# When the row sums of a gated feed-forward layer enter GpSimd's queue: at once, or two TensorE products later

## The chip, the cores and the metric

The kernel runs on one core of a Trainium2 chip. The metric is the time of one execution on the device in microseconds (us). TensorE multiplies matrices out of the on-chip memory SBUF into PSUM banks; VectorE (DVE), ScalarE (ACT) and GpSimd (POOL) do the elementwise work; SyncE (SP) and GpSimd issue most of the DMA transfers to and from HBM. Each engine takes its own instructions in order; between engines semaphores make one wait for another.

## The reference

One layer of a trunk over 2048 tokens of width 1024, in float32:

```python
xn = rmsnorm(x, norm1_g)
z = xn @ w_in                        # pooling branch, HGRN2 branch, gates
...
x = x + merged @ w_o
x = x + conv_glu_ffn(rmsnorm(x, norm2_g), w_up, conv_w, conv_b, w_down)
return rmsnorm(x, final_g)

def conv_glu_ffn(x, w_up, conv_w, conv_b, w_down):
    h = x @ w_up                     # 1024 -> 2 x 2816
    hp = pad(h, CONV_WIDTH - 1)      # two tokens of history
    hc = sum(conv_w[j] * hp[:, j:j + S] for j in range(3)) + conv_b
    val, gate = split(hc, 2)
    return (silu(gate) * val) @ w_down
```

The change is in the last part, the feed-forward layer (up-projection, causal convolution over three tokens, SiLU gate, down-projection).

## The kernel before

**Blocks and halves.** The tokens are worked off in two blocks of 1024 (`b0` = 0 and 2 in the names: `h0_...`, `h2_...`). Each block goes first through the mixer (input projection, pooling, HGRN2, output projection), then through the feed-forward layer. There a block is two halves of 512 tokens, `hf` 0 and 1. Channels lie on the 128 partitions, tokens along the free axis, so one tile is 128 x 512.

**Units and products.** The up-projection has 22 units per block; unit `m` makes 128 channels of the value (`s` = 0) and the same 128 of the gate (`s` = 1) for both halves. These four tiles form a 2 x 2 matrix product, done with seven products in place of eight (Strassen's way), in the order P1, P6, P5, P7, P2, P4, P3. A product is twelve matmuls of 128 x 512: four steps along the width, each with three terms, because both operands are split into a high and a low part. Three PSUM banks hold them: X takes P1 and P2, Z takes P6, P7 and P4, V takes P5 and P3. Products add up in a bank, and in between partial results are read out: after P1 ScalarE copies X to `e1` (L992); after P6 VectorE makes `u2` = `e1` - Z (L994), and P7, which goes on adding in Z, waits for that read; after P7 `u3` = Z - `e1` (L998). The four tiles `h(s,hf)` come out as h(1,1) after P7 (VectorE, L958), h(0,0) after P2 (ScalarE, L952), h(1,0) after P4 (L956) and h(0,1) after P3 (VectorE, L958).

**Behind a tile.** `conv` takes `h(s,hf)`: GpSimd copies the two columns that lie before it, the halo (L1339: from the history if `hf` is 0, otherwise from the end of half 0) and, with `hf` 1, its own last two columns into the history (L1341). ScalarE starts `e` with the token's own weight and the bias (L1344), and VectorE adds the first and the second tap, the tokens one and two places earlier (L1346, L1348). `glu` makes the gated row: SiLU on ScalarE (L1352), then the product on VectorE (L1354 for half 1, L1356 for half 0; for units 0 to 3 the half-0 product is GpSimd's, since `G_POOL` is 4). `glu(0)` runs after P4, `glu(1)` after P3.

**Sums of rows.** The down-projection is again done with seven products, over pairs of units `k` = m // 2. Its seven operands are three gated rows themselves (P1: half 1 of the even unit; P2: half 1 of the odd unit; P4: half 0 of the odd unit) and four sums of rows, P7, P5, P6, P3, which `add_forms` makes on GpSimd (L1064, tiles `gf{b0}_{P}_{k}`): P7 once the even unit is complete, P5 and P6 (= P5 minus a row) behind the odd unit's first half, P3 (= P6 plus a row) behind its second. Each is stored to HBM (`dg...`): the sums by a DMA from GpSimd's queue right behind each sum (L1368), the rows by a list that SP works off at the next product. The down-projection fetches them back through GpSimd's queue (`g...`, L776) and splits each into a high and a low part (`dn_P_kh` by L577 on ScalarE, `dn_P_kl` by L578 on VectorE); its first steps are split while the last unit still runs.

**What sets the order.** `up_order` puts units 0 and 1, and 2 and 3, next to one another, product by product (the head pairs); units 4 to 21 follow one after another. Weights come as raw tiles by SP (8 buffers) and are split by L204 on ScalarE and L205 on VectorE up to four tiles ahead. A scheduler of the framework simulates the program and gives each engine its final order from the order in which the code issues instructions and from dependencies; so code that is issued later may come later on the engine, among whatever is ready. `in_turn(ins)` gives an instruction a dependency for this scheduling alone, on the latest matmul: in the scheduler's order it comes after that matmul, and no semaphore is waited for in the program.

All matmuls are recorded at one line (L145). The engine rows name tiles without their buffer numbers: `up_Z`, `h`, `e`, `gf_P`, `dg_P`, `ops` (a split weight tile), `raw` (a loaded one).

Of the kernel before, what the change touches and what calls it, by code (L numbers as in the profile page):

```python
# [69 lines left out]
N_RAW = 8  # L70
GROUP = 4
SUM_LAG = 7
N_OPS = 6
LOOKAHEAD = 4
MM_PER_TICK = 6
# [3 lines left out]
def tile_trunk(  # L79
# [16 lines left out]
    pe, act, dve, pool, sp = nc.tensor, nc.scalar, nc.vector, nc.gpsimd, nc.sync  # L96
# [3 lines left out]
    rawp = ctx.enter_context(tc.tile_pool(name="rawp", bufs=N_RAW))  # L100
    opsp = ctx.enter_context(tc.tile_pool(name="opsp", bufs=N_OPS))
    slots = ctx.enter_context(tc.tile_pool(name="slots", bufs=N_SLOTS))
# [138 lines left out]
    class Sums:  # L241
# [12 lines left out]
        def make(self, g):  # L254
# [4 lines left out]
            for dst, src, add in (("s1", 2, 0), ("s3", 2, 0), ("s1", 3, 1), ("s3", 0, 1),  # L259
# [4 lines left out]
                else:  # L264
                    with tc.issue_after(stream.mark.ins):
                        act.dma_start(self.t[g, dst], x)
                yield SUM_LAG
            self.done.add(g)
# [158 lines left out]
    sums = {}  # L427
# [627 lines left out]
                        step(j, k, ws[n])  # L1055
                stream.used(hold)

    def add_forms(two, forms, k, name, store=lambda p, t: None):

        def comb(p, x0, x1, op):  # L1060
            if (p, k) in forms or x0 is None or x1 is None:
                return
            t = slot(f"{name}_{p}_{k}")
            pool.tensor_tensor(t, x0, x1, op)  # L1064
            forms[p, k] = t
            store(p, t)

        for p, at in (("P1", (1, 0)), ("P2", (1, 1)), ("P4", (0, 1))):
            if (p, k) not in forms and at in two:
                forms[p, k] = two[at]  # L1070
                store(p, two[at])
        comb("P7", two.get((1, 0)), two.get((0, 0)), ALU.subtract)
        comb("P5", two.get((0, 0)), two.get((0, 1)), ALU.subtract)
        comb("P6", forms.get(("P5", k)), two.get((1, 0)), ALU.subtract)
        comb("P3", forms.get(("P6", k)), two.get((1, 1)), ALU.add)
# [247 lines left out]

    def ffn(b0, forms, late):
        gd, gt, gp = {}, {}, {}
        stores = []

        def flush():
            for d, g in stores:
                sp.dma_start(d, g)  # L1330
            stores.clear()

        def emit_up(m):
            hs, ts = {}, {}

            def conv(s, hf):
                mt = m + MF * s
                h = hs[s, hf]
                pool.tensor_copy(h[:, 0:2], hist[:, mt] if hf == 0 else hs[s, 0][:, TB : TB + 2])  # L1339
                if hf == 1:  # L1340
                    pool.tensor_copy(hist[:, mt], h[:, TB : TB + 2])  # L1341
                t = slot(f"e{b0}_{m}_{s}_{hf}")
                ts[s, hf] = t
                act.activation(t, h[:, 2:], AF.Identity, bias=col(o_cb + mt),  # L1344
                               scale=col(o_cw + 4 * MF + mt))
                dve.scalar_tensor_tensor(t, h[:, 1 : 1 + TB], col(o_cw + 2 * MF + mt), t,  # L1346
                                         ALU.mult, ALU.add)
                dve.scalar_tensor_tensor(t, h[:, 0:TB], col(o_cw + mt), t, ALU.mult, ALU.add)  # L1348

            def glu(hf):  # L1350
                g = ts[1, hf]
                act.activation(g, g, AF.Silu)  # L1352
                if hf:
                    dve.scalar_tensor_tensor(g, g, -1.0, ts[0, hf], ALU.mult, ALU.mult)  # L1354
                else:
                    (pool if m < G_POOL else dve).tensor_tensor(g, g, ts[0, hf], ALU.mult)  # L1356
                k = m // 2
                two = gp.setdefault(k, {})
                two[hf, m % 2] = g

                def store(p, t):
                    name = f"dg{b0}_{p}_{k}"
                    d = dram.tile([P, TB], F32, tag=name, name=name)
                    gd[p, k] = d
                    if p in R_FORM:
                        stores.append((d, t))
                    else:
                        pool.dma_start(d, t)  # L1368

                add_forms(two, gt, k, f"gf{b0}", store)  # L1370

            def emit(s, hf, a, ps):
                h = slot(f"h{b0}_{m}_{s}_{hf}", 2 + TB)
                hs[s, hf] = h
                value(h[:, 2:], a, ps)
                first = (0, 0) if m >= 2 * N_HEADS else (1, 0)
                if (s, hf) == first:
                    conv(0, 0)
                if (s, hf) == (1, 0):
                    conv(1, 0)  # L1380
                    glu(0)
                elif (s, hf) == (0, 1):
                    conv(0, 1)
                    conv(1, 1)
                    glu(1)

            return emit

        acc = {}
        fg = []  # L1390
        fss = {}

        def load_acc(which):
            for hf, c in which:
                for j in range(NT):
                    acc[hf, j, c] = fetch(x2d[b0 + hf, j, c], f"ac{b0}_{hf}_{j}_{c}", pool)

        def square(hf, j, c):
            if (hf, j) not in fss:
                fss[hf, j] = small.tile([P, 4], F32, tag="fss", name=f"fss{b0}_{hf}_{j}")  # L1400
            act.activation(slot(f"fj{b0}_{hf}_{j}_{c}"), acc[hf, j, c], AF.Square,
                           accum_out=fss[hf, j][:, c : c + 1])

        def final(hf, j):
            if hf == 1 and not last:
                yield FIN_WAIT
            for c in range(2):
                square(hf, j, c)
            halves = [acc.pop((hf, j, c)) for c in range(2)]
            res = [slot(f"fo{b0}_{hf}_{j}_{c}") for c in range(2)]  # L1410
            ss = fss[hf, j]
            pool.tensor_tensor(ss[:, 2:3], ss[:, 0:1], ss[:, 1:2], ALU.add)
            r = rstd_of(ss[:, 2:3], 1, 1.0 / D, f"f{b0}_{hf}_{j}r")
            yield 3
            rr = (b0 + hf) * TB + j * P
            for c in (1 - hf, hf):
                if (hf, c) == (0, 1):
                    act.activation(res[c], halves[c], AF.Copy, scale=r[:, 0:1])
                    pool.tensor_tensor(res[c], res[c], fg[c], ALU.mult)
                else:  # L1420
                    dve.scalar_tensor_tensor(res[c], halves[c], r[:, 0:1], fg[c],  # L1421
                                             ALU.mult, ALU.mult)
                sp.dma_start(out[rr : rr + P, 512 * c : 512 * c + 512], res[c])

        down = Rows(f"dn{b0}", "dn", DOWN, MF // 2,
                    lambda p, k: fetch(gd[p, k], f"g{b0}_{p}_{k}", pool), acc, 5)
        EARLY = {"P7": 2, "P4": 3}
        units = {}
        for n, (m, p) in enumerate(up_order()):
            if n == GO_AT:  # L1430
                go_up[0] = True
            if m not in units:
                units[m] = Unit(f"up{b0}_{m}", "up", emit_up(m))
            u = units[m]
            u.multiply(p, forms, late)
            if p != "P3":
                flush()
            u.after(p)
            if m == MF - 1 and p in EARLY:
                down.make(EARLY[p])  # L1440

        last = b0 + 2 >= SEQ // TB
        nxt = []

        def each0(k):
            if k in (3, 5, 7):
                load_acc((((1, 1), (0, 0), (0, 1))[(k - 3) // 2],))

        def each1(k):
            if k == 5:  # L1450
                load_acc(((1, 0),))

        def each2(k):
            if k == 2:
                for h in range(2):
                    t = slot(f"fg{b0}_{h}")
                    sp.dma_start(t, final_g[512 * h : 512 * h + 512].partition_broadcast(P))
                    fg.append(t)

        def each3(k):  # L1460
            if k == X_AT and not last:
                load_rows(b0 + 2)
                nxt.append(forms_of("x", b0 + 2, o_n1, go=lambda: go_io[0]))
            if k == X_AT2 and not last:
                load_rows(b0 + 3)

        down.make(3)
        flush()
        down.run("P1", 0, each0)
        down.run("P6")  # L1470
        down.run("P2", 0, each1)
        down.run("P7")
        down.run("P5", 0, each2)
        down.run("P4", 2, done=lambda j: Task(final(0, j)))
        go_io[0] = False
        down.run("P3", 6 if last else 3, each3, lambda j: Task(final(1, j)))
        return nxt[0] if nxt else None
# [15 lines left out]
    for b in range(0, SEQ // TB, 2):  # L1493
        forms, task, late = nxt
        join(task)
        forms, task, late = mixer(b, forms, late)
# [52 lines left out]
```

## Time and profile before

| | |
|---|---|
| time, median of 3 runs | 2761.86 us (2761.05 to 2764.86) |
| profiled execution, its own time | 2769.87 us |
| its span | 2767.9 us |
| mean granted clock of TensorE | 0.969 |
| bytes moved | 515.75 MB, mean 186 GB/s |
| sums of rows (L1064), mean of one | 1.328 us (two rows), 1.311 us (a sum and a row) |
| halo copies (L1339), mean of one | 0.534 us, x88 |
| stores of the sums (`dg_P<-gf_P`) | x88, 256 KB, 2.7 us from issue to landing |

The profiled execution lies 2.0 us above its span: that is what stands before the first and behind the last recorded instruction. A line of the page's list of groups reads: line, engine, operation, out<-in (partitions x elements, type), count | busy time, mean ns of one | idle time of the engine just before these instructions, and who ended most of it. In a timeline row the first two numbers are start and duration in us (with `xN` at the end: N instructions together), and the bracket at the end is the idle time before it and who released it.

### The profile page before, as it was taken

The numbers are of one execution on the slowest core, as the hardware profiler recorded it, in microseconds if no ns is written. First come the engines' busy times: TensorE is split into PE (matmuls) and PEld (weight loads), VectorE is DVE, ScalarE is ACT, GpSimd is POOL, SyncE is SP. The second block draws the span as 40 slices with busy tenths as digits, with TensorE's granted clock in tenths as the row PEclk, the third lists the DMA queues.
The fourth block names the chain that finished last, engine by engine and source line by source line (L and its number), as shares of the span: only waits on it lengthen the run. The fifth ranks groups of instructions, "written<-read, shape, count | busy, mean of one in ns | idle before, by whom it ended". The sixth has DMA issues, their size and how long they took to land. (4 is left out here: it accounts for less than half of the span.)

```text
span 2767.9 us, 35412 instructions
## 1 busy us (share of the span) xinstructions
PE 2581.0 (93%) x11464; PEld 2085.2 (75%) x11464; DVE 1932.8 (70%) x3390; ACT 1166.4 (42%) x2204; POOL 907.0 (33%) x1273
## 2 busy tenths in 40 slices
PE   7899999889979999989989999999998899998998
PEld 5677887667767777767868788888776677776886
DVE  6888878368876766666577787775877666667744
ACT  5333434224534444434464344442354444444533
POOL 5544343072443233343252111202333322224412
PEclk8999999999989999999999999999999999999999
DMA  5656666879677787899888444346343443435943
GB/s 201 212 145 166 173 167 184 259 235 262 159 184 200 204 217 222 222 298 351 257 239 240 124 122 130 121 153 236 123 138 101 128 127 124 141 119 175 345 148 103
DMA packets 258313, 515.75 MB, mean 186 GB/s; under 512 B 26224, under 2 KB 42736, under 8 KB 257648
## 3 DMA queue, kind: packets, MB, share of 16 engines
q1 hardware_dynamic: 177600, 301.01, 33.8%
q0 software_dynamic: 51040, 129.52, 19.5%
q10 hardware_dynamic: 29488, 82.96, 8.5%
q8 instruction: 90, 1.47, 0.2%
q14 instruction: 95, 0.78, 0.1%
HBM read 422.69 MB, written 206.05 MB: 227 GB/s over the span
## 5 line engine op out<-in xcount | busy, mean ns | idle before, releaser
L204 ACT CAST ops<-raw 128x512 fp32r<-128x512 f32 x732 | 451.5, 620 | 951.6 <-PE dn_P L145 161.3
L205 DVE TENSOR_TENSOR ops<-raw,ops 128x512 fp32r<-128x512 f32 x732 | 534.4, 733 | 324.0 <-ACT ops L204 312.6
L1344 ACT ACTIVATE e<-h,cols 128x512 f32<-128x512 f32 x176 | 138.5, 812 | 45.4 <-DVE h L958 38.4
L1346 DVE SCALAR_TENSOR_TENSOR e<-h,cols,e 128x512 f32<-128x512 f32 x176 | 130.9, 765 | 31.9 <-POOL h L1339 21.5
L1348 DVE SCALAR_TENSOR_TENSOR e<-h,cols,e 128x512 f32<-128x512 f32 x176 | 129.9, 752 | 0.6
L776 POOL DMA_DIRECT2D g_P<-dg_P x154 | 85.1, 558 | 136.7 <-PE dn_P L145 76.8
L1064 POOL TENSOR_TENSOR gf_P<-e,e 128x512 f32<-128x512 f32 x44 | 58.4, 1328 | 193.5 <-DVE e L1354 128.1
L145 PE MATMUL up_Z<-m_T30h,ops 128*128 128x512 f32 x88 | 42.1, 478 | 77.1 <-DVE up_u L994 77.1
L998 DVE TENSOR_TENSOR up_u<-up_Z,up_e 128x512 f32<-128x512 f32 x44 | 30.4, 691 | 116.5 <-PE up_Z L145 116.5
L1339 POOL COPY h<-h 128x2 f32<-128x2 f32 x88 | 45.9, 534 | 154.1 <-DVE h L956 154.1
L145 PEld LDWEIGHTS up_Z<-m_T30h,ops 128*128 128x128 f32 x88 | 18.0, 205 | 93.7 <-DVE up_u L994 76.3
L1064 POOL TENSOR_TENSOR gf_P<-gf_P,e 128x512 f32<-128x512 f32 x44 | 57.7, 1311 | 85.0 <-DVE e L1354 84.6
L1273 POOL TENSOR_TENSOR ya<-ya,gl 128x512 f32<-128x512 f32 x32 | 46.2, 1473 | 111.8 <-DVE gl L1265 110.3
L1341 POOL COPY hist<-h 128x2 f32<-128x2 f32 x88 | 28.1, 319 | 167.1 <-DVE h L958 166.9
L1206 ACT ACTIVATE gt<-gt,cols 128x512 f32<-128x512 f32 x48 | 34.8, 725 | 78.6 <-DVE gt L958 60.1
L1352 ACT ACTIVATE e<-e 128x512 f32<-128x512 f32 x88 | 55.2, 627 | 29.3 <-DVE e L1348 28.2
L1040 DVE TENSOR_TENSOR ac<-ac,dn_P 128x512 f32<-128x512 f32 x72 | 46.7, 683 | 27.4 <-PE dn_P L145 20.1
L825 POOL COPY qm<-q 128x64 f32<-128x64 f32 x64 | 25.5, 411 | 121.3 <-DVE q L849 25.0
L1169 POOL TENSOR_TENSOR q<-q,qs 128x512 f32<-128x512 f32 x16 | 21.9, 1367 | 128.8 <-ACT qs L1168 78.0
L958 DVE TENSOR_TENSOR h<-up_u,up_V 128x512 f32<-128x512 f32 x88 | 60.1, 683 | 2.8 <-PE up_V L145 2.3
L1040 DVE TENSOR_TENSOR x<-x,wo_P 128x512 f32<-128x512 f32 x88 | 55.9, 676 | 7.2 <-PE wo_P L145 7.2
L952 ACT COPY h<-up_X 128x512 f32<-128x512 f32 x44 | 25.8, 587 | 80.0 <-PE up_X L145 80.0
(1270 smaller groups left out, 8382.0 us busy)
## 6 DMA issues: line engine op xcount, KB each, us to landing
g_P<-dg_P POOLq DMA_DIRECT2D x154, 256.0 KB, 7.0
raw<-in_w_up_t SPq DMA_DIRECT2D x132, 256.0 KB, 3.0
raw<-in_w_in_t SPq DMA_DIRECT2D x98, 256.0 KB, 2.9
dg_P<-gf_P POOLq DMA_DIRECT2D x88, 256.0 KB, 2.7
raw<-in_w_io SPq DMA_DIRECT2D x68, 256.0 KB, 5.3
dg_P<-e SPq DMA_DIRECT2D x66, 256.0 KB, 3.2
raw<-in_w_dn SPq DMA_DIRECT2D x66, 256.0 KB, 5.4
x<-in_x SPq DMA_DIRECT2D x64, 256.0 KB, 5.4
```

What stands on the lines that cost most here:

```text
L145: count[1] = pe.matmul(*args, **kw)
L204: self.mark = act.copy(hi, v)
L205: dve.tensor_tensor(lo, v, f32(hi), ALU.subtract)
L776: eng.dma_start(t, d)
L958: dve.tensor_tensor(dst, t, ps, ALU.add if how == "add" else ALU.subtract)
L1040: dve.tensor_tensor(t, t, ps[j], ALU.add if sg > 0 else ALU.subtract)
L1064: pool.tensor_tensor(t, x0, x1, op)
L1273: pool.tensor_tensor(y[m, hf], y[m, hf], g, ALU.add)
L1344: act.activation(t, h[:, 2:], AF.Identity, bias=col(o_cb + mt), scale=col(o_cw + 4 * MF + mt))
L1346: dve.scalar_tensor_tensor(t, h[:, 1 : 1 + TB], col(o_cw + 2 * MF + mt), t, ALU.mult, ALU.add)
L1348: dve.scalar_tensor_tensor(t, h[:, 0:TB], col(o_cw + mt), t, ALU.mult, ALU.add)
L1352: act.activation(g, g, AF.Silu)
```

## The change

The rows P1, P2 and P4 are entered and their stores listed at once as before. The four sums, with the stores behind them, are put on a list and issued two products later (`FORM_LAG`), right after the matmuls of that product are issued, each sum pinned by `in_turn` behind the last of these matmuls in the scheduler's order. `have` is a copy of the pair's rows as they were when the sums were put off, so that the same sums are made at each place. What is left on the list after the last unit is issued there. `add_forms` has another caller (other operands of the layer), which passes neither argument and so works as before.

```diff
 SUM_LAG = 7
+FORM_LAG = 2
...
-    def add_forms(two, forms, k, name, store=lambda p, t: None):
+    def add_forms(two, forms, k, name, store=lambda p, t: None, sums=True, pin=lambda i: None):
 
         def comb(p, x0, x1, op):
             if (p, k) in forms or x0 is None or x1 is None:
                 return
             t = slot(f"{name}_{p}_{k}")
-            pool.tensor_tensor(t, x0, x1, op)
+            pin(pool.tensor_tensor(t, x0, x1, op))
             forms[p, k] = t
             store(p, t)
...
                 store(p, two[at])
+        if not sums:
+            return
         comb("P7", two.get((1, 0)), two.get((0, 0)), ALU.subtract)
...
     def ffn(b0, forms, late):
         gd, gt, gp = {}, {}, {}
+        later, turn = [], [0]
         stores = []
...
-                add_forms(two, gt, k, f"gf{b0}", store)
+                have = dict(two)
+                add_forms(have, gt, k, f"gf{b0}", store, False)
+                later.append((turn[0] + FORM_LAG, lambda: add_forms(
+                    have, gt, k, f"gf{b0}", store, True, in_turn)))
...
             u.multiply(p, forms, late)
+            turn[0] = n
+            while later and later[0][0] <= n:
+                later.pop(0)[1]()
             if p != "P3":
                 flush()
             u.after(p)
...
+        for _, fn in later:
+            fn()
         last = b0 + 2 >= SEQ // TB
```

Behind the change the line numbers are shifted: L1339 becomes L1343, L1341 L1345, L1064 L1065, L1346 L1350, L1348 L1352, L1354 L1358, L1356 L1360, L1368 L1372, L958 L959, L994 L995, L205 L206.

On GpSimd, around the end of unit 9 in the second block (names are `h2_9_0_1`: block, unit, value or gate, half; the tail is a buffer number). Before:

```order
L1339 COPY h2_9_1_1_20302<-h2_9_1_0_20345 128x2
L1064 TENSOR_TENSOR gf2_P5_4_20355<-e2_8_1_0_20180,e2_9_1_0_20348 128x512
L1368 DMA dg2_P5_4_20357<-gf2_P5_4_20355 128x512
L1064 TENSOR_TENSOR gf2_P6_4_20359<-gf2_P5_4_20355,e2_8_1_1_20213 128x512
L1339 COPY h2_9_0_1_20380<-h2_9_0_0_20321 128x2
L1341 COPY hist_121<-h2_9_0_1_20380 128x2
L1368 DMA dg2_P6_4_20361<-gf2_P6_4_20359 128x512
L1064 TENSOR_TENSOR gf2_P3_4_20397<-gf2_P6_4_20359,e2_9_1_1_20390 128x512
L1368 DMA dg2_P3_4_20399<-gf2_P3_4_20397 128x512
```

and now:

```order
L1343 COPY h2_9_1_1_20302<-h2_9_1_0_20345 128x2
L1343 COPY h2_9_0_1_20372<-h2_9_0_0_20321 128x2
L1345 COPY hist_121<-h2_9_0_1_20372 128x2
L1065 TENSOR_TENSOR gf2_P5_4_20407<-e2_8_1_0_20180,e2_9_1_0_20348 128x512
L1372 DMA dg2_P5_4_20409<-gf2_P5_4_20407 128x512
L1065 TENSOR_TENSOR gf2_P6_4_20411<-gf2_P5_4_20407,e2_8_1_1_20213 128x512
L1372 DMA dg2_P6_4_20413<-gf2_P6_4_20411 128x512
L1065 TENSOR_TENSOR gf2_P3_4_20437<-gf2_P6_4_20411,e2_9_1_1_20382 128x512
L1372 DMA dg2_P3_4_20439<-gf2_P3_4_20437 128x512
```

The halo copy of the value's second half, `h2_9_0_1`, and the history copy behind it stood behind sums P5 and P6; now they stand ahead of P5.

On VectorE, at the same place, from the product of the first half to `u2` of unit 10. Before:

```order
L1356 TENSOR_TENSOR e2_9_1_0_20348<-e2_9_1_0_20348,e2_9_0_0_20324 128x512
L205 TENSOR_TENSOR ops649_20450<-raw635_20255,ops649_20450 128x512
L958 TENSOR_TENSOR h2_9_0_1_20380<-up2_9_u2_20263,up2_9_V_20265 128x512
L1346 SCALAR_TENSOR_TENSOR e2_9_0_1_20384<-h2_9_0_1_20380,cols_84,e2_9_0_1_20384 128x512
L1346 SCALAR_TENSOR_TENSOR e2_9_1_1_20390<-h2_9_1_1_20302,cols_84,e2_9_1_1_20390 128x512
L205 TENSOR_TENSOR ops650_20467<-raw636_20275,ops650_20467 128x512
L1348 SCALAR_TENSOR_TENSOR e2_9_0_1_20384<-h2_9_0_1_20380,cols_84,e2_9_0_1_20384 128x512
L1348 SCALAR_TENSOR_TENSOR e2_9_1_1_20390<-h2_9_1_1_20302,cols_84,e2_9_1_1_20390 128x512
L205 TENSOR_TENSOR ops651_20488<-raw637_20292,ops651_20488 128x512
L1354 SCALAR_TENSOR_TENSOR e2_9_1_1_20390<-e2_9_1_1_20390,e2_9_0_1_20384 128x512
L994 TENSOR_TENSOR up2_10_u2_20441<-up2_10_e1_20421,up2_10_Z_20423 128x512
```

and now, from the read of bank V on:

```order
L959 TENSOR_TENSOR h2_9_0_1_20372<-up2_9_u2_20263,up2_9_V_20265 128x512
L1352 SCALAR_TENSOR_TENSOR e2_9_1_0_20348<-h2_9_1_0_20345,cols_84,e2_9_1_0_20348 128x512
L206 TENSOR_TENSOR ops648_20426<-raw634_20230,ops648_20426 128x512
L1350 SCALAR_TENSOR_TENSOR e2_9_0_1_20376<-h2_9_0_1_20372,cols_84,e2_9_0_1_20376 128x512
L1350 SCALAR_TENSOR_TENSOR e2_9_1_1_20382<-h2_9_1_1_20302,cols_84,e2_9_1_1_20382 128x512
L1352 SCALAR_TENSOR_TENSOR e2_9_0_1_20376<-h2_9_0_1_20372,cols_84,e2_9_0_1_20376 128x512
L1360 TENSOR_TENSOR e2_9_1_0_20348<-e2_9_1_0_20348,e2_9_0_0_20324 128x512
L1352 SCALAR_TENSOR_TENSOR e2_9_1_1_20382<-h2_9_1_1_20302,cols_84,e2_9_1_1_20382 128x512
L206 TENSOR_TENSOR ops649_20450<-raw635_20251,ops649_20450 128x512
L206 TENSOR_TENSOR ops650_20467<-raw636_20275,ops650_20467 128x512
L1358 SCALAR_TENSOR_TENSOR e2_9_1_1_20382<-e2_9_1_1_20382,e2_9_0_1_20376 128x512
L995 TENSOR_TENSOR up2_10_u2_20441<-up2_10_e1_20417,up2_10_Z_20419 128x512
```

The read of bank V (`h2_9_0_1`), both first taps of the second half (L1350) and one second tap now come before the product of the first half (L1360, formerly L1356), and the weight tiles `ops649` and `ops650` now stand behind them.

On GpSimd, in the first head pair (units 0 and 1) of the second block. Before:

```order
L1339 COPY h2_1_1_1_18945<-h2_1_1_0_18995 128x2
L1356 TENSOR_TENSOR e2_0_1_0_18972<-e2_0_1_0_18972,e2_0_0_0_18967 128x512
L1356 TENSOR_TENSOR e2_1_1_0_19003<-e2_1_1_0_19003,e2_1_0_0_18998 128x512
L1064 TENSOR_TENSOR gf2_P5_0_19010<-e2_0_1_0_18972,e2_1_1_0_19003 128x512
L1339 COPY h2_0_0_1_19031<-h2_0_0_0_18570 128x2
L1341 COPY hist_121<-h2_0_0_1_19031 128x2
L1368 DMA dg2_P5_0_19012<-gf2_P5_0_19010 128x512
L1064 TENSOR_TENSOR gf2_P7_0_19048<-e2_0_1_1_19041,e2_0_1_0_18972 128x512
L1064 TENSOR_TENSOR gf2_P6_0_19052<-gf2_P5_0_19010,e2_0_1_1_19041 128x512
L1339 COPY h2_1_0_1_19073<-h2_1_0_0_18589 128x2
```

and now:

```order
L1343 COPY h2_1_1_1_18945<-h2_1_1_0_18995 128x2
L1343 COPY h2_0_0_1_19027<-h2_0_0_0_18570 128x2
L1360 TENSOR_TENSOR e2_0_1_0_18972<-e2_0_1_0_18972,e2_0_0_0_18967 128x512
L1345 COPY hist_121<-h2_0_0_1_19027 128x2
L1360 TENSOR_TENSOR e2_1_1_0_19003<-e2_1_1_0_19003,e2_1_0_0_18998 128x512
L1065 TENSOR_TENSOR gf2_P5_0_19061<-e2_0_1_0_18972,e2_1_1_0_19003 128x512
L1343 COPY h2_1_0_1_19065<-h2_1_0_0_18589 128x2
L1372 DMA dg2_P5_0_19063<-gf2_P5_0_19061 128x512
L1345 COPY hist_121<-h2_1_0_1_19065 128x2
L1065 TENSOR_TENSOR gf2_P7_0_19100<-e2_0_1_1_19037,e2_0_1_0_18972 128x512
L1065 TENSOR_TENSOR gf2_P6_0_19104<-gf2_P5_0_19061,e2_0_1_1_19037 128x512
```

The halo copy of unit 0 now stands ahead of both of GpSimd's products, and that of unit 1 directly behind P5 and no longer behind P7 and P6.

## The prediction

> **What bounds the kernel now.** I read the page first (TensorE's share), then the chain of waits, the waits in total, and the engines' timelines around one stall.
>
> ```profile
> span 2767.9 us, 35412 instructions
> PE 2581.0 (93%) x11464; PEld 2085.2 (75%) x11464; DVE 1932.8 (70%) x3390; ACT 1166.4 (42%) x2204; POOL 907.0 (33%) x1273
> ```
>
> TensorE is busy for 93% of the span, so a change that removes no product can only win the time in which TensorE waits or runs slowly. The profiled execution took 2769.87 us, 8.0 above the median of 2761.86 (0.29%); differences are taken from the profile and set against the median.
>
> ```profile
> PE up_Z L145 <- DVE up_u L994: 77.1, 20, 8.8
> ```
>
> This row of the waits (total us, times, longest) is TensorE's largest. It always strikes at the same place: the first matmul of P7 of an even unit, which continues bank Z and so waits until VectorE has read P6 out of it (`u2`, L994). The chain over one such stall, between units 7 and 8 of the second block (start us, us, what):
>
> ```profile
> 2231.89 2.79 PE up_V L145 x12
> ...
> 2236.05 0.68 DVE e L1356
> 2236.80 1.31 POOL gf_P L1064
> 2238.40 0.56 POOL dg_P L1368
> 2238.98 1.31 POOL gf_P L1064
> 2240.30 0.13 POOL h L1339
> 2240.45 0.65 DVE e L1346
> 2242.39 1.42 DVE e L1348 x2
> 2243.83 0.64 ACT e L1352
> 2244.50 0.69 DVE e L1354
> 2245.19 0.61 DVE up_u L994
> ```
>
> Read backwards: `u2` stands behind the convolution of the odd unit's second half, that waits for a two-column copy `h` (0.13 us, L1339), and the copy stands in GpSimd's queue behind the sums P5 and P6 and a store, which wait for the first half's product (L1356). The copy itself needs nothing of this.
>
> The stalls on TensorE's timeline (start us, us, ..., idle before in brackets):
>
> ```profile
> 721.84 0.50 PE L145 MATMUL up_Z<-m_T23h,ops 128*128 128x512 f32 x1 [1.85 <-ACT m_T23h L577]
> ...
> 2121.61 0.77 PE L145 MATMUL up_Z<-m_T30h,ops 128*128 128x512 f32 x1 [7.16 <-DVE up_u L994]
> 2158.43 0.79 PE L145 MATMUL up_Z<-m_T30h,ops 128*128 128x512 f32 x1 [8.75 <-DVE up_u L994]
> 2289.53 0.50 PE L145 MATMUL up_Z<-m_T30h,ops 128*128 128x512 f32 x1 [2.82 <-DVE up_u L994]
> 2504.84 0.51 PE L145 MATMUL up_Z<-m_T30h,ops 128*128 128x512 f32 x1 [2.79 <-DVE up_u L994]
> 2542.57 2.12 PE L145 MATMUL dn_P<-ops,dn_P_2h 128*128 128x512 f32 x8 [1.23 <-ACT dn_P_2h L577]
> 2550.84 3.76 PE L145 MATMUL dn_P<-ops,dn_P_3h 128*128 128x512 f32 x8 [4.87 <-ACT dn_P_3h L577]
> ```
>
> Per block these are two long stalls behind the head pairs (units 0, 1 and 2, 3), eight of about 2.8 us behind units 5, 7, ... 19, and 1.23 + 4.87 us where the down projection starts. Twenty stalls make the 77.1 us.
>
> The stall also costs TensorE its clock. The chain gives the twelve matmuls of P7 right behind the eight pair stalls of the second block:
>
> ```profile
> 2202.14 4.62 PE up_Z L145 x12
> 2245.84 4.33 PE up_Z L145 x12
> 2289.53 3.05 PE up_Z L145 x12
> 2331.66 4.61 PE up_Z L145 x12
> 2375.36 3.05 PE up_Z L145 x12
> 2417.51 4.62 PE up_Z L145 x12
> 2461.18 4.58 PE up_Z L145 x12
> 2504.84 3.03 PE up_Z L145 x12
> ```
>
> Five of the eight took about 1.5 us more than the other three. The 1.85 us gap at 721.84 is followed by 0.50 us for its first matmul, as at 2289.53, where the twelve were fast (at 2121.61 it is 0.77): I take gaps under about 1.9 us as harmless.
>
> **The change part by part.** The counts stay: 88 sums, 88 stores of them, the copies. Moved are, per odd unit, the second half's halo copy and history copy ahead of sums P5 and P6 in GpSimd's queue; on VectorE the subtraction `h` that empties bank V, which now stands directly behind the first tap of the first half; on ScalarE the two activations L1344 of the second half ahead of the first half's SiLU; on SP one store ahead of one weight load; on GpSimd a few accumulating weight DMAs ahead of a store. The pin is an order and no wait. The SP and DMA moves I cost at nothing: loads run up to eight tiles ahead. If that cover were gone, each would cost at most one product's time, 2.8 us.
>
> What the new order meets is contention between GpSimd's sums and VectorE. Of the first head pair:
>
> ```profile
> 2101.12 1.88 DVE L1348 SCALAR_TENSOR_TENSOR e<-h,cols,e 128x512 f32<-128x512 f32 x1
> 2104.18 0.74 DVE L1348 SCALAR_TENSOR_TENSOR e<-h,cols,e 128x512 f32<-128x512 f32 x1
> ...
> 2101.15 1.30 POOL L1356 TENSOR_TENSOR e<-e,e 128x512 f32<-128x512 f32 x1 [0.68 <-ACT e L1352]
> ```
>
> The same instruction takes 1.88 us beside a GpSimd operation on two tiles (of the form of the sums) and 0.74 us without: it ends 0.55 us after that does. Today the pairs' sums run while VectorE idles or reads PSUM, so nothing collides. In the new order the sums fall beside two-input SBUF work.
>
> The walk, for units 9 and 10 on the clock of these rows (VectorE's starts lie 0.60 us apart, those of L1346 and L1348 0.67):
>
> ```profile
> 2277.97 0.39 PE L145 MATMUL up_V<-m_B223h,ops 128*128 128x512 f32 x1
> 2286.31 0.40 PE L145 MATMUL up_V<-m_T13h,ops 128*128 128x512 f32 x1
> ...
> 2282.44 0.68 DVE L958 TENSOR_TENSOR h<-up_u,up_V 128x512 f32<-128x512 f32 x1
> ...
> 2281.17 0.62 ACT L204 CAST ops<-raw 128x512 fp32r<-128x512 f32 x1 [1.49 <-PE up_X L145]
> 2283.22 1.52 ACT L1344 ACTIVATE e<-h,cols 128x512 f32<-128x512 f32 x2 [1.42 <-DVE h L958]
> 2287.53 0.63 ACT L1352 ACTIVATE e<-e 128x512 f32<-128x512 f32 x1 [0.16 <-DVE e L1348]
> ...
> 2282.09 0.56 POOL L1368 DMA_DIRECT2D dg_P<-gf_P  x1 [0.30 <-POOL gf_P L1064]
> ```
>
> P3 is complete at 2278.36; `h` can start at 2278.4 instead of 2282.44. Then: second tap 2279.0, a weight tile 2279.7, first taps of the second half 2280.3 and 2280.9, second tap 2281.6, first half's product 2282.3 (its SiLU is done by 2281.2), second tap 2282.9 to 2283.6. Sum P5 waits for that and holds VectorE's next weight tile until 2284.8; that tile ends at 2285.35, the next runs to 2285.9. Sum P6, 0.30 + 0.56 us behind P5, takes 2285.9 to 2287.1 and holds the second half's product (SiLU ready 2285.1): 2287.7. `u2` follows to 2288.3 and P7 starts there: 1.2 us before the 2289.53 of today, 1.7 us after the work in front of it. Without any collision `u2` would end at 2286.5, and P7 is due at 2286.54: no stall.
>
> - Pairs: 16 x 1.2 = 19 us. Ends: 0 (collisions take all) and 16 x 2.8 = 45. I take the walk.
> - Clock: 5 of 8 in each block, 10 x 1.5 = 15 us, if a 1.7 us gap no longer trips it. Ends 0 and 15. I take 15, by the gap at 721.84.
> - Heads: the stalls sum to 15.9 us in this block, so about 32 in both. GpSimd still multiplies there, and the second copy still stands behind P5, but no longer behind P7 and P6. The first stall may lose some 4 of 7 us. At the second, P7 comes one product sooner after the pair, and VectorE's rows leave `u2` behind everything: 0.4. Twice 4.4 = 9, and 3 of clock. Ends 0 and 32.
> - Start of the down projection: the split of row 3 stands behind unit 21's last SiLU, which comes earlier by the same means (I walk it to about 2546 instead of 2550.18): 4 of 6.1 us, and half a microsecond of clock; 9 in both. Ends 0 and 12.
>
> Sum 19 + 15 + 12 + 9 = 55; 2762 - 55 = **2707 us**.
>
> [...]
>
> **The rivals.**
> - Fewer collisions. If sum P6 comes after the product has started, one blocking goes: P7 1.2 us earlier, 2707 - 16 x 1.1 = 2689. If none blocks, another 0.6 us a pair and some 9 at the heads: 2670. For it: 0.2 us decides who of P6 and the product comes first. Against it: the row at 2101.12 had VectorE 0.03 us ahead and it still lost.
> - The slow clock stays, because 1.7 us is near what tripped it: 2707 + 15 = 2722. For it: 1.85 us is one gap only.
> - The sums take all back: each pair keeps 2.8 us and its clock; the heads and the down projection alone give 21: 2741.
> - Slower: the blocking grows. A third blocked instruction on the same chain (sum P3 of the unit before, or P7 on the even one) costs another 1.2 us and brings P7 to 2289.5, today's time; with a fourth it is 1.2 us worse than today: 16 x 1.2 + 6 x 1.5 = 28, less 12 from the down projection and heads: 2778. It decides from the third collision on. Against it: in the walk P3 falls beside `u2`, which reads PSUM, and rows such as L958 show no lengthening there.
> - Nothing comes of it, since the moved copy was only the last of several reasons: 2762, within 0.2% (5.5 us), which is what a measurement here can tell from no change.
>
> **How the numbers follow.** Forecast 45% (2697 to 2717); fewer collisions 21%; slow clock 14%; all taken back 8%; no change 6%; slower 6%. Faster is the first four, 0.88; same 0.06; slower 0.06. The range from 2672 to 2740 leaves out no change, slower, and the edges of the second and fourth case.
>
> **What the profile would show.** Right: the copy (L1343 there) no longer waits behind `gf_P`; the idle time before P7 falls from 2.8 to about 1.7 us on 16 places; `up_Z` x12 rows behind them are all near 3.05; VectorE's product L1358 (formerly L1354) and one weight tile L206 in each pair lengthen to over 1.2 us; the first head stall moves to unit 3 or shrinks to about 3 us; `dn_P_3h` waits 1 to 2.5 us. Wrong: L1358 keeps 0.69 us and the gaps vanish (fewer collisions); the gaps stay at 2.8 us with the copy early (the sums took it); 4.6 us rows persist behind short gaps (clock); a new stall of TensorE in odd units (slower).

## The result, and the profile after

The changed kernel takes 2725.68 us (median of 4 runs, 2724.83 to 2727.51), the kernel before beside it 2762.97 us (4 runs, 2761.05 to 2764.86): a ratio of 0.9866, 95% interval [0.9849, 0.9883], 37.3 us less. The forecast was 2707 us in a range of 2672 to 2740; the direction came true, and two thirds of the gain. The profiled execution took 2727.51 us.

From the page of the changed kernel, the lines that are shown of the kernel before:

```profile
span 2725.0 us, 35432 instructions
PE 2568.9 (94%) x11464; PEld 2077.4 (76%) x11464; DVE 1990.4 (73%) x3390; ACT 1166.1 (43%) x2204; POOL 963.7 (35%) x1273
```

and from its waits in total (us, times, longest):

```profile
PE up_Z L146 <- DVE up_u L995: 53.8, 20, 8.3
...
PE dn_P L146 <- ACT dn_P_10h L578: 7.4, 1, 7.4
```

VectorE does the same 3390 instructions and is busy 57.6 us longer, GpSimd 56.7 us longer: both hold one another up more than before. TensorE's wait for `u2` fell from 77.1 to 53.8 us, at still 20 places. The stalls on TensorE's timeline (start, us, ..., idle before in brackets): first the two head stalls, then two ordinary pairs and an odd one out, then stalls of the down projection, two of the first block and one of the second:

```profile
2097.19 0.47 PE L146 MATMUL up_Z<-m_T30h,ops 128*128 128x512 f32 x1 [2.92 <-DVE up_u L995]
2127.90 0.76 PE L146 MATMUL up_Z<-m_T30h,ops 128*128 128x512 f32 x1 [8.24 <-DVE up_u L995]
2171.64 0.50 PE L146 MATMUL up_Z<-m_T30h,ops 128*128 128x512 f32 x1 [2.05 <-DVE up_u L995]
2254.47 0.50 PE L146 MATMUL up_Z<-m_T30h,ops 128*128 128x512 f32 x1 [2.05 <-DVE up_u L995]
1009.87 0.50 PE L146 MATMUL up_Z<-m_T30h,ops 128*128 128x512 f32 x1 [0.47 <-DVE up_u L995]
...
1175.53 0.50 PE L146 MATMUL dn_P<-ops,dn_P_3h 128*128 128x512 f32 x1 [1.75 <-ACT dn_P_3h L578]
1221.67 0.80 PE L146 MATMUL dn_P<-ops,dn_P_6h 128*128 128x512 f32 x1 [5.86 <-ACT dn_P_6h L578]
2507.99 0.50 PE L146 MATMUL dn_P<-ops,dn_P_3h 128*128 128x512 f32 x1 [3.97 <-ACT dn_P_3h L578]
```

Fifteen of the sixteen pair stalls are 2.04 to 2.08 us (2.8 to 3.0 before), one is 0.47. What holds `u2` there, around the stall at 2254.47 (VectorE and GpSimd), and behind it the same instructions ahead of the short stall at 1009.87:

```profile
2249.25 0.69 DVE L206 TENSOR_TENSOR ops<-raw,ops 128x512 fp32r<-128x512 f32 x1
2250.33 1.31 DVE L206 TENSOR_TENSOR ops<-raw,ops 128x512 fp32r<-128x512 f32 x1 [0.40 <-ACT ops L205]
2251.56 2.25 DVE L1358 SCALAR_TENSOR_TENSOR e<-e,e 128x512 f32<-128x512 f32 x1
2253.74 0.67 DVE L995 TENSOR_TENSOR up_u<-up_e,up_Z 128x512 f32<-128x512 f32 x1
...
2248.75 2.34 POOL L1065 TENSOR_TENSOR gf_P<-e,e 128x512 f32<-128x512 f32 x1 [3.23 <-DVE e L1360]
2251.97 1.28 POOL L1065 TENSOR_TENSOR gf_P<-gf_P,e 128x512 f32<-128x512 f32 x1
...
1008.54 0.68 DVE L1358 SCALAR_TENSOR_TENSOR e<-e,e 128x512 f32<-128x512 f32 x1
1009.14 0.67 DVE L995 TENSOR_TENSOR up_u<-up_e,up_Z 128x512 f32<-128x512 f32 x1
...
1008.96 1.40 POOL L1065 TENSOR_TENSOR gf_P<-gf_P,e 128x512 f32<-128x512 f32 x1
```

Sum P5 starts at 2248.75 and takes 2.34 us; a weight tile takes 1.31 in place of 0.69, the second half's product L1358 takes 2.25 in place of 0.69, and `u2` stands right behind it. At 1008.54 product and sum P6 lie the same way, yet the product takes 0.68: that one collision less is 2.05 - 0.47 = 1.6 us.

By stage, from the starts of the first matmul of unit 0, of unit 5, of the down projection and the end of the latter (us, first block / second block):

| | units 0 to 4 | units 5 to 21 | down projection | the two mixers |
|---|---|---|---|---|
| before | 128.1 / 129.8 | 366.9 / 364.4 | 242.6 / 222.7 | 691.6 / 612.2 |
| changed | 124.7 / 124.4 | 351.5 / 354.0 | 241.4 / 219.8 | 689.0 / 610.5 |
| less | 8.8 | 25.8 | 4.1 | 4.3 |

The two mixers hold none of the instructions that moved; their 4.3 us are a difference between two profiles of equal work. The two spans differ by 42.9 us, the medians by 37.3.

### The profile page after: what moved, and what is told of

Its sections match the earlier page's. It is cut to its first block, busy times and chain, and to the rows that moved or that the text cites. A ratio compares the mean times of both kernels' runs of the same rounds, so it can differ in the third digit from the quotient of the medians.

```text
span 2725.0 us, 35432 instructions
## 1 busy us (share of the span) xinstructions
PE 2568.9 (94%) x11464; PEld 2077.4 (76%) x11464; DVE 1990.4 (73%) x3390; ACT 1166.1 (43%) x2204; POOL 963.7 (35%) x1273
## 5 line engine op out<-in xcount | busy, mean ns | idle before, releaser
L205 ACT CAST ops<-raw 128x512 fp32r<-128x512 f32 x732 | 451.2, 620 | 932.6 <-PE up_Z L146 241.5
L206 DVE TENSOR_TENSOR ops<-raw,ops 128x512 fp32r<-128x512 f32 x732 | 563.4, 773 | 300.7 <-ACT ops L205 292.5
L1348 ACT ACTIVATE e<-h,cols 128x512 f32<-128x512 f32 x176 | 138.6, 813 | 19.3 <-DVE h L959 8.6
L1352 DVE SCALAR_TENSOR_TENSOR e<-h,cols,e 128x512 f32<-128x512 f32 x176 | 144.3, 825 | 0.0
L1065 POOL TENSOR_TENSOR gf_P<-e,e 128x512 f32<-128x512 f32 x44 | 77.8, 1769 | 171.8 <-DVE e L1358 113.0
L1350 DVE SCALAR_TENSOR_TENSOR e<-h,cols,e 128x512 f32<-128x512 f32 x176 | 134.6, 787 | 3.4
L1343 POOL COPY h<-h 128x2 f32<-128x2 f32 x88 | 54.2, 642 | 152.8 <-DVE h L957 152.8
L1345 POOL COPY hist<-h 128x2 f32<-128x2 f32 x88 | 40.7, 462 | 180.3 <-DVE h L959 180.0
L146 PE MATMUL up_Z<-m_T30h,ops 128*128 128x512 f32 x88 | 39.6, 450 | 53.8 <-DVE up_u L995 53.8
L1356 ACT ACTIVATE e<-e 128x512 f32<-128x512 f32 x88 | 54.9, 624 | 32.9 <-DVE e L1352 32.8
L959 DVE TENSOR_TENSOR h<-up_u,up_V 128x512 f32<-128x512 f32 x88 | 60.2, 684 | 5.4 <-PE up_V L146 3.9
L1065 POOL TENSOR_TENSOR gf_P<-gf_P,e 128x512 f32<-128x512 f32 x44 | 59.0, 1340 | 11.0 <-DVE e L1358 10.3
L1372 POOL DMA_DIRECT2D dg_P<-gf_P x88 | 55.6, 632 | 19.3 <-POOL gf_P L1065 18.7
```

What stands on the lines that cost most here:

```text
L146: count[1] = pe.matmul(*args, **kw)
L205: self.mark = act.copy(hi, v)
L206: dve.tensor_tensor(lo, v, f32(hi), ALU.subtract)
L959: dve.tensor_tensor(dst, t, ps, ALU.add if how == "add" else ALU.subtract)
L1065: pin(pool.tensor_tensor(t, x0, x1, op))
```

## The experiments

Theory A, as in the prediction: the sums' place in GpSimd's queue made the stall, and what is left is their contention with VectorE. Each kernel was timed beside the kernel before, on the same chip.

| | median, us | kernel before beside it | ratio, 95% |
|---|---|---|---|
| copy alone | 2769.84 (10 runs) | 2763.07 (13) | 1.0025 [1.0009, 1.0042] |
| thin sums | 2662.17 (4) | 2763.07 (13) | 0.9635 [0.9605, 0.9666] |
| lag 3 | 2666.91 (4) | 2763.07 (13) | 0.9671 [0.9635, 0.9707] |
| lag 5 | 2661.86 (4) | 2763.07 (13) | 0.9632 [0.9606, 0.9659] |
| lag 2, u2 first | 2671.00 (4) | 2765.56 (7) | 0.9662 [0.9639, 0.9686] |
| sums on VectorE | 2712.86 (4) | 2765.56 (7) | 0.9812 [0.9795, 0.9829] |
| lag 5, no si0 | 2648.48 (4) | 2765.56 (7) | 0.9581 [0.9564, 0.9598] |
| lag 5, hold | 2640.85 (4) | 2765.56 (7) | 0.9556 [0.9541, 0.9571] |
| u2 first, sums at once | 2671.99 (4) | 2766.20 (7) | 0.9663 [0.9640, 0.9687] |
| lag 2, hold | 2720.86 (4) | 2766.20 (7) | 0.9838 [0.9819, 0.9856] |

**1. The copy alone.** The kernel before; only the halo copy of `h(0,1)` is issued ahead of `glu(0)`.

```diff
...
                     conv(1, 0)
+                    g = hs[0, 1] = slot(f"h{b0}_{m}_0_1", 2 + TB)
+                    pool.tensor_copy(g[:, 0:2], hs[0, 0][:, TB : TB + 2])
                     glu(0)
```

> The kernel before, with one thing moved: the halo copy of h(0,1) is issued ahead of the first half's product and sums, everything else (the sums at once, no lag) stays. Theory A (the copy behind the sums is the whole reason of the stall before P7): the gap before P7 falls from 2.8 us to about 2 us or less on 16 places as in the changed kernel, 2725 to 2735 us. Theory B (the copy is only the last of several things in that place; what wins is that the whole second half, the read of bank V, its activations and taps, gets ahead of the first half's product and of the sums): the gap stays at 2.7 to 3.0 us, the second head stall at about 9 us, 2755 to 2765 us. I hold B here, since ScalarE still has the first half's SiLU ahead of the second half's activations, and a replay of the order puts the gap at 2.96 us.

It became 0.25% slower, 4.8 us above the range of Theory B, which was held. GpSimd's copy now runs early (L1384), and the stall grew to 3.19 us:

```profile
2280.21 0.66 POOL L1384 COPY h<-h 128x2 f32<-128x2 f32 x1
2286.51 1.30 POOL L1064 TENSOR_TENSOR gf_P<-gf_P,e 128x512 f32<-128x512 f32 x1
...
2284.82 1.52 ACT L1345 ACTIVATE e<-h,cols 128x512 f32<-128x512 f32 x2
2286.11 2.93 DVE L1347 SCALAR_TENSOR_TENSOR e<-h,cols,e 128x512 f32<-128x512 f32 x2
...
2293.00 0.50 PE L145 MATMUL up_Z<-m_T30h,ops 128*128 128x512 f32 x1 [3.19 <-DVE up_u L994]
```

ScalarE still makes the second half's activations only at 2284.82, and the first taps then meet sum P6 (2.93 us for two that take 1.41 alone). The copy that the chain of waits named was only the last of several reasons.

**2. Thin sums.** The changed kernel; each sum is made on 32 of its 512 columns, and its store takes a row in its place.

```diff
-            pin(pool.tensor_tensor(t, x0, x1, op))
+            thin = name[:2] == "gf"
+            n = 32 if thin else TB
+            pin(pool.tensor_tensor(t[:, :n], x0[:, :n], x1[:, :n], op))
...
-            store(p, t)
+            store(p, x0 if thin and p in ("P7", "P5") else x1 if thin else t)
```

> The changed kernel, with the sums made on 32 of 512 columns, and the stores of the sums taking an operand of the sum in their place: what is left out is 15/16 of the sums' arithmetic; the number of instructions and of bytes stays, and VectorE's order in units 0 to 20 too. Theory A (what is left of the stall is GpSimd's sums and VectorE's two-input operations holding one another up): the 2.05 us gaps before P7 vanish, L1358 keeps 0.69 us, the second head stall falls from 8.3 to 3.5 to 5 us, the stall at dn_P_3h shrinks by 2 us; 2725.7 - 16 x 2.05 - 3 x 1.5 - 2 x 4 - 4 = about 2676 us (2665 to 2690). Rival (VectorE has that much work in the pair, the sums do not matter): gaps stay at 2 us, 2720 to 2727 us.

All pair gaps vanish, and the second head stall falls from 8.2 to 4.7 us; units 5 to 21 take 334.6 and 334.2 us. VectorE's order there is that of the changed kernel, and its product takes its own time (L1360 in this kernel, `u2` behind it):

```profile
2242.27 0.69 DVE L206 TENSOR_TENSOR ops<-raw,ops 128x512 fp32r<-128x512 f32 x1 [0.42 <-ACT ops L205]
2242.88 0.69 DVE L1360 SCALAR_TENSOR_TENSOR e<-e,e 128x512 f32<-128x512 f32 x1
2243.48 0.68 DVE L995 TENSOR_TENSOR up_u<-up_e,up_Z 128x512 f32<-128x512 f32 x1
```

So the remaining 2.05 us were contention, not VectorE's amount of work. The time, 2662.17 us, lies 2.8 us under the range that was expected.

**3 and 4. Longer lags.**

```diff
-FORM_LAG = 2
+FORM_LAG = 3      (experiment 4: 5)
```

> The changed kernel with the sums issued three products later instead of two. Theory A (collision of the sums with VectorE's chain to u2 makes the 2.05 us gap): sums P5 and P6 come behind that chain, the pair gaps fall under 0.8 us, the second head stall to 5.6 us; by a replay of its order 18 us a block, 2 x 18 + 4 for clock: about 2685 us (2675 to 2700). Rival (VectorE's amount of work sets the gap): 2720 to 2728 us. Rival (later sums delay the stores and the fetches of the down projection): a stall of more than 6 us at its start, 2700 to 2720 us.

> The sums five products later. Theory A: as three products, and the second head stall falls to about 2.6 us: by the replay 22 us a block less than the changed kernel, with 4 for clock about 2676 us (2665 to 2690). Rival (VectorE's amount of work): 2720 to 2728 us. Rival (the last pair's sums come so late that the down projection waits): 2690 to 2720 us, with the gain of the pairs given back behind P1 of the down projection.

Both gained 14 to 18 us more than expected, and for another reason than mine. Part of the gain is given back in the first block's down projection, which takes 244.3 us (lag 3) and 247.5 (lag 5) in place of 241.4. With lag 5:

```profile
2243.46 2.34 POOL L1065 TENSOR_TENSOR gf_P<-e,e 128x512 f32<-128x512 f32 x1 [3.23 <-DVE e L1360]
2246.67 1.31 POOL L1065 TENSOR_TENSOR gf_P<-gf_P,e 128x512 f32<-128x512 f32 x1
...
2244.55 0.69 DVE L995 TENSOR_TENSOR up_u<-up_e,up_Z 128x512 f32<-128x512 f32 x1
2245.15 1.20 DVE L206 TENSOR_TENSOR ops<-raw,ops 128x512 fp32r<-128x512 f32 x1
2246.27 2.27 DVE L1358 SCALAR_TENSOR_TENSOR e<-e,e 128x512 f32<-128x512 f32 x1
```

The sums are no later (P5 starts 0.78 us behind the start of the first half's product, as with lag 2; with both lags that product ends 3.23 us of idle time on GpSimd there), and they collide as before. What changed is VectorE's order: `u2` now stands ahead of L1358, so the blocking hits nothing that P7 waits for. Units 5 to 21 take 331.0 and 330.7 us.

**5. u2 first, lag 2.** The test of that reading: the second half's `glu` is issued three products later and its product ordered behind the next unit's `u2`; the sums stay two products late.

```diff
-                dve.tensor_tensor(self.tmp("u2"), t["e1"], bk["Z"], ALU.subtract)
+                count[2] = dve.tensor_tensor(self.tmp("u2"), t["e1"], bk["Z"], ALU.subtract)
...
-                    dve.scalar_tensor_tensor(g, g, -1.0, ts[0, hf], ALU.mult, ALU.mult)
+                    behind(dve.scalar_tensor_tensor(g, g, -1.0, ts[0, hf], ALU.mult, ALU.mult), count[2])
...
-                    glu(1)
+                    later.append((turn[0] + 3, lambda: glu(1)))
...
```

> The changed kernel, sums still two products late, with the second half's product L1358 put behind u2 of the next unit in VectorE's queue (issued three products later, and ordered behind u2). GpSimd's sums P5 and P6 stand where they stand in the changed kernel, so they go on colliding. Theory A' (after e3 and e4: what the 2.05 us gap needs is that u2 stands behind the held-up product L1358; the later lags only put u2 ahead of it, the sums come as early as before): the pair gaps fall under 0.8 us though L1358 still takes about 2.2 us; by a replay of the order 18 us a block and 4 for clock: about 2682 us (2670 to 2695). Rival (it is the sums' time that counts, and the longer lag moved that): gaps stay at 1.5 to 2 us, 2710 to 2727 us.

Confirmed: the pair stalls are gone (332.1 and 331.7 us), with the product still held up (1.66 us, where 2.2 were expected):

```profile
2254.50 0.68 DVE L995 TENSOR_TENSOR up_u<-up_e,up_Z 128x512 f32<-128x512 f32 x1
2255.09 1.66 DVE L1358 SCALAR_TENSOR_TENSOR e<-e,e 128x512 f32<-128x512 f32 x1
...
2254.90 1.29 POOL L1065 TENSOR_TENSOR gf_P<-gf_P,e 128x512 f32<-128x512 f32 x1
```

**6. Sums on VectorE.**

```diff
-            pin(pool.tensor_tensor(t, x0, x1, op))
+            pin((dve if sums and name[0] == 'g' else pool).tensor_tensor(t, x0, x1, op))
```

> The changed kernel with the 88 sums made by VectorE in place of GpSimd, two products late as before. Nothing collides any more (but GpSimd's products of the heads), and VectorE has 88 x 0.6 = 53 us more to do. Theory A (blocking, not the amount of work, made the gap): L1358 and the weight tiles keep 0.69 us, but each pair has two or three sums ahead of u2 at 0.6 us: gaps of about 1.4 us in even units and 0.7 in odd ones, 2715 to 2735 us. Rival (VectorE has slack enough in a pair): gaps vanish, 2665 to 2690 us.

A little better than the range that I gave. The product keeps 0.69 us; the sums now stand ahead of `u2` themselves, and the stalls have the sizes of the expectation:

```profile
2201.07 1.41 DVE L1065 TENSOR_TENSOR gf_P<-gf_P,e 128x512 f32<-128x512 f32 x2
2203.14 0.50 PE L146 MATMUL up_Z<-m_T30h,ops 128*128 128x512 f32 x1 [1.35 <-DVE up_u L995]
2223.50 0.47 PE L146 MATMUL up_Z<-m_T30h,ops 128*128 128x512 f32 x1 [0.68 <-ACT ops L205]
```

The second row, of an odd unit, ends with a weight tile of ScalarE; `u2` was done 0.12 us before it, so the sum ahead of `u2` is not the whole reason there.

**9. u2 first, sums at once.** Experiment 5 without any lag of the sums: GpSimd's queue around them as in the kernel before, the copy behind P5 and P6.

```diff
-                add_forms(have, gt, k, f"gf{b0}", store, False)
-                later.append((turn[0] + FORM_LAG, lambda: add_forms(
-                    have, gt, k, f"gf{b0}", store, True, in_turn)))
+                add_forms(two, gt, k, f"gf{b0}", store)
```

> The order of sums and copies of the kernel before (sums at once, halo copy of h(0,1) behind sums P5 and P6), with one thing changed: the second half's product (L1354 there, L1358 here) is issued three products later and ordered behind u2 of the next unit in VectorE's queue. Theory A' (P7 only needs u2 to stand ahead of what waits for the second half; neither the sums' time nor the copy's place matters then): pair gaps under 0.8 us, 331 to 336 us for the pairs of a block, 2670 to 2700 us. Rival (the halo copy has to get ahead of the sums, as the prediction read the chain of waits): VectorE still waits for the copy ahead of u2, gaps of 1.5 to 2.5 us, 2720 to 2745 us.

This refutes the prediction's reading of the chain, that the copy had to get ahead of the sums. 94 us are won with the copy where it always stood:

```profile
2245.95 1.31 POOL L1065 TENSOR_TENSOR gf_P<-gf_P,e 128x512 f32<-128x512 f32 x1
2247.19 0.20 POOL L1343 COPY h<-h 128x2 f32<-128x2 f32 x1
...
2247.42 1.42 DVE L1350 SCALAR_TENSOR_TENSOR e<-h,cols,e 128x512 f32<-128x512 f32 x2 [1.01 <-POOL h L1343]
2248.75 0.68 DVE L995 TENSOR_TENSOR up_u<-up_e,up_Z 128x512 f32<-128x512 f32 x1
...
2249.56 0.39 PE L146 MATMUL up_V<-m_T13h,ops 128*128 128x512 f32 x1
2249.79 0.40 PE L146 MATMUL up_Z<-m_T30h,ops 128*128 128x512 f32 x1
```

VectorE even waits 1.01 us for the copy, but `u2` follows right behind the first taps, ahead of the second taps and the product, and P7 starts without a gap. Units 5 to 21: 331.0 and 330.6 us.

The edit moves more than the expectation names: all of `glu(1)` is issued later, its SiLU too. `u2` needs bank Z and ScalarE's copy `e1`, and in the kernel before ScalarE made `e1` right behind the second half's SiLU, which waits for the second taps. The copy before, ending at 2288.63 just ahead of `u2` at 2288.80, and in experiment 9:

```profile
2288.06 0.57 ACT L992 COPY up_e<-up_X 128x512 f32<-128x512 f32 x1
...
2247.93 0.57 ACT L993 COPY up_e<-up_X 128x512 f32<-128x512 f32 x1
```

By these two times, moving `u2` alone on VectorE would have won some 0.2 us a pair at most (an estimate); `e1` had to get out from behind the SiLU as well. No run moves one without the other.

**7, 8 and 10. The down projection.** The fetches of its rows stand in GpSimd's queue among accumulating transfers of 1 MB that add up the next block's weights. In the changed kernel, on GpSimd's timeline ahead of the stall at 1221.67:

```profile
1217.56 0.55 POOL L777 DMA_DIRECT2D g_P<-dg_P  x1 [7.01 <-DMA si0s<-in_w_in_t]
```

and in the list of DMA issues (KB each, median us from issue to landing):

```profile
si0s<-in_w_in_t POOLq DMA_DIRECT2D x4, 1024.0 KB, 16.5
```

Experiment 7 (lag 5) leaves the first group of them out; experiments 8 (lag 5) and 10 (lag 2) hold them all until P1 and P6 of the first block's down projection are issued. The edit of 7, then that of 8 and 10:

```diff
-                if add:
+                if add and self.name == "si" and g == 0:
+                    pass
+                elif add:
```

```diff
                 x = self.t[g, src] if isinstance(src, str) else self.groups[g][1][src]
+                while hold[0]:
+                    yield 1
...
+        hold[0] = b0 == 0
         down.make(3)
         flush()
         down.run("P1", 0, each0)
         down.run("P6")
+        hold[0] = False
```

> Sums five products late, without the four accumulating transfers of 1 MB each that add up the first group of input-projection weights (left out: these additions, 4 MB of traffic). The question is the stall of 6 us at dn_P_6h in the first block's down projection, where a fetch of a row stands in GpSimd's queue until the transfer si0s<-in_w_in_t has landed (8.3 us of idle). Theory (that landing is the cause): the stall falls under 2 us and the first block's down projection takes 247.5 - 6 = 241 us or less; about 2655 us (2648 to 2660). Rival (the fetches are slow in any case, as the rows' stores and loads are all in flight there): the stall stays over 4 us, 2658 to 2665 us.

> Sums five products late, and the accumulating transfers of the next block's weight sums wait (in the order of issue) until P1 and P6 of the first block's down projection are issued; nothing is left out. Theory as for the run without them: stall at dn_P_6h under 2 us, 2652 to 2658 us, if the transfers don't collide with later fetches. Rival: the stall moves to a later product of the down projection or to the next block's projections, 2660 to 2670 us.

> The changed kernel (sums two products late) with the accumulating transfers of the weight sums held until P1 and P6 of the first block's down projection are issued. Theory (the missing gain of the down projection in the prediction was taken back at dn_P_6h by such a transfer): the pairs keep their 2.05 us gaps, the stall of 5.9 us at dn_P_6h goes, the first block's down projection takes 231 to 235 us in place of 241.4; 2715 to 2720 us. Rival (in the changed kernel the fetches are late for another reason): down projection over 239 us, 2723 to 2728 us.

Without the group the stall at `dn_P_6h` falls from 6.07 to 3.59 us, not under 2, and the first block's down projection from 247.5 to 241.3 us: the landing is part of the cause. Held, that stall is gone with either lag, and the first block's down projection takes 231.2 us (lag 5) and 231.6 (lag 2), a gain of 16.3 and 9.8 us; experiment 8 lies 11 us under its expected range, experiment 10 just above its own. The longer stall at `dn_P_10h` near its end, 7.4 us in the waits above, became two of 3 us; with lag 5:

```profile
1338.03 0.50 PE L147 MATMUL dn_P<-ops,dn_P_7h 128*128 128x512 f32 x1 [3.00 <-ACT dn_P_7h L581]
...
1353.66 0.50 PE L147 MATMUL dn_P<-ops,dn_P_10h 128*128 128x512 f32 x1 [3.06 <-ACT dn_P_10h L581]
```

Experiment 10's time, 2720.86, is only 4.8 us below the changed kernel's though its down projection is 9.8 us shorter: its second mixer took 5.7 us longer (616.2). Whether that mixer pays for the held transfers is open; with lag 5 it took 610.5. Experiment 8, 2640.85 us, is the best version, 124.7 us below the kernel before.

Without the pin (`in_turn` left away) the order of all five engines is the same row by row, so none of this is the pin's doing.

## Why the prediction was right, and where it was wrong

- **The place of the gain and what limits it** were right: the stalls before P7, shortened and not removed, since sums P5 and P6 now meet VectorE; L1358 and one weight tile lengthen as named; the first head stall moves to unit 3 with 3 us (2.92 measured, 3.08 in the first block); the second stays (8.24).
- **Pairs, forecast 19 us.** The step that failed is "sum P5 waits for that and holds VectorE's next weight tile until 2284.8". P5 did not get through behind the second tap: the tap and the weight tile at 2249.25 kept their 0.74 and 0.69 us, and P5, which ended 1.15 us after VectorE fell idle at 2249.94, took 2.34. Sum P6 came 0.35 us later than walked, the product and P7 some 0.4 us, on a clock that fits the walk to 0.1 us up to there. From stall to stall of two fast pairs it was 42.13 us (2289.53 to 2331.66) and is 41.40 (2171.64 to 2213.04): 0.73 less, not 1.2. Over 16 pairs the missing 0.47 us make 7.5 us of the difference.
- **Clock, forecast 15 us.** Eleven slow P7 (six in the first block, where the prediction took five) became three, 8 x 1.5 = 12 us. The one gap of 1.85 us was too thin a basis: three of the fifteen gaps of 2.04 to 2.08 us still had a slow P7 behind them, and where a gap lay on the grid of the clock's records counted as well (below).
- **Heads, forecast 12 us:** 8.8. The four stalls shrank by 9 us as forecast (31.5 to 22.6); the 3 us of clock did not come.
- **Start of the down projection, forecast 9 us:** 4.1, and this term failed because it put nothing for the fetches behind the first steps. In the first block 1.23 + 4.87 became 1.75 + 0.90, nearly as walked; then the stall at `dn_P_6h`, 2.28 before, grew to 5.86 us, because the fetch that stands behind the transfer came only 1.9 us sooner after the stage's start (52.3 us behind it, before 54.2). Experiment 10 shows that the transfers make it: with them held, the stall is gone. In the second block 3.97 us remain (1.75 with thin sums), where the last unit's second taps meet sums P5 and P6:

```profile
2502.82 3.95 DVE L1352 SCALAR_TENSOR_TENSOR e<-h,cols,e 128x512 f32<-128x512 f32 x2
```

- **Profile and median.** The stages give 38.7 us where 55 were forecast, and the medians 37.3. The profile of before lay 6.9 us over its median, that of the changed kernel 1.8, so the two profiles differ by more than the medians; 4.3 us of their difference lie in the mixers. What compares with the forecast's terms is the 38.7.
- **The rivals.** 2725.68 lies outside the 2697 to 2717 of the forecast's own case. It is near the 2722 of "the slow clock stays", but not by it: most of the clock came back. "Fewer collisions" came true at one pair of sixteen (1009.87), and its price of 1.1 us was 1.6.
- **What no part of the prediction saw:** that the copy was not the key. One rival allowed for it, but only to expect no gain. The chain of waits ran back from `u2` through what VectorE does ahead of it. I asked what holds that work, and not why `u2` and its operand `e1`, which need nothing of the convolution, stand behind it. Experiment 9, which moves both ahead, gains 94 us; experiment 1, which moves what the chain named, loses 7.

## What to carry to other kernels

When a chain of waits passes through an instruction that only stands behind another in its engine's queue, try first to move the waiting instruction ahead, together with the operands that it needs; only then speed up what is in front. A lag or a pin that is meant to move one engine's work may move nothing there and reorder another engine: compare the orders, then look which instruction really stood aside. And work that comes sooner runs into the next queue: look what the transfers behind it wait for.

## What the runs showed of the hardware

**The clock and the length of a gap.** The twelve matmuls of P7 right behind a pair stall take 3.05 us or 4.2 to 4.6, in the changed kernel for example:

```profile
2254.47 3.05 PE up_Z L146 x12
...
2295.88 4.58 PE up_Z L146 x12
```

Slow were 3 of 15 behind gaps of 2.04 to 2.08 us (changed kernel) and 11 of 16 behind 2.79 to 3.02 (before). The length of a gap alone does not sort them: in the changed kernel the twelve matmuls behind 2.92 us of a head stall (2097.19) took 3.02 us, those behind 2.06 us (2295.88) took 4.58.

The records of the granted clock show more. In the profiles of before and of the changed kernel it is full (1.00) or half (0.50), and up to the last record every stretch of one clock lasts a whole multiple of 3.413 us, so that it changes only on a grid of that step. These are the two stretches of that grid that hold the gaps before the rows above, each with the one that follows (us, TensorE busy, granted clock, DMA share, GB/s):

```profile
2252.61:2256.02 3.41, 1.55 (x7) 1.00 0.79 287
2256.02:2259.43 3.41, 3.41 (x16) 1.00 0.48 165
2293.57:2296.98 3.41, 1.35 (x7) 1.00 0.69 259
2296.98:2300.39 3.41, 3.41 (x10) 0.50 0.56 203
```

The gap before 2295.88 lies whole within one stretch, 2.06 us idle, and the next is granted half the clock. The gap before 2254.47 began 0.19 us ahead of its stretch, which so has 1.86 us idle, and the clock stays. Over these two profiles, a stretch at full clock was followed by one at half after 0 of 1441 with less than 1.4 us idle, 11 of 31 with 1.4 to 2.0, and 43 of 43 with 2.0 or more (the ends of matmuls are modelled, so the bounds are rough). So in these profiles the place of a gap on the grid counted as well as its length.

**Who blocks whom.** At 2251.56 VectorE's product began 0.41 us ahead of sum P6 and ended 0.56 us behind it; at 1008.54 it began 0.42 us ahead and was not held at all (0.68 us), and the sum took 1.40 us. Of the changed kernel's 44 products L1358, 27 lay beside no sum and took 0.68 to 0.69 us; of the 17 beside one, 16 took 2.25 to 2.29 and that of 1008.54 took 0.68. `u2`, which reads PSUM, took 0.67 to 0.68 us at all 40 places where it lay beside a sum. Which of two was issued first could not be read from the recorded starts.

**Profiles of equal work.** Up to the feed-forward layer of the first block all kernels run the same order; in the profiles that layer's first matmul on bank Z, the start of P6 of unit 0, comes at 710.8 (lag 5), 714.9 (changed) and 717.5 us (before). Differences of that size between two profiles have to be taken out by stage before one reads them as an effect.
